# Means over the features in the head norms: one full fp32 matmul, or two one-pass matmuls of two exact parts

## The chip, the cores and the metric

The kernel runs on one core of one Trainium2 chip. The metric is the device time of one execution in microseconds (us). The engines are TensorE (PE in the profile; PEld is its weight load), VectorE (DVE), ScalarE (ACT), GpSimd (POOL) and SyncE (SP). Each engine works through its own instructions strictly in program order and waits on semaphores where an instruction needs another engine's result.

## The reference, cut to what matters

One inference step of a decoder layer with 512 prompt tokens and 8 decoding tokens, 2048 features, all in fp32. One projection gives the columns of three head groups: A, an HGRN2 recurrence (4 heads); B, sliding-window attention (8 heads); C, a retention (4 heads). Groups A and C end in a norm over the 128 features of a head, times a gate:

```python
def head_rms_norm(o, g):                       # group A
    y = o * lax.rsqrt(jnp.mean(o * o, axis=-1, keepdims=True) + NORM_EPS)
    return y * g

def head_group_norm(o, g):                     # group C
    c = o - jnp.mean(o, axis=-1, keepdims=True)
    y = c * lax.rsqrt(jnp.mean(c * c, axis=-1, keepdims=True) + NORM_EPS)
    return y * g

o_a = head_rms_norm(o_a, a_gain) * silu(ga)
o_c = head_group_norm(o_c, c_gain) * silu(gc)
mix = concatenate([o_a, o_b, o_c]); x = x + mix @ w_out
x = x + conv_ffn(rms_norm(x))                  # 2048 -> 2 x 5632 -> 2048
```

## The kernel before, in words

**Layout.** Features lie on the 128 partitions, tokens along the free dimension: 520 columns (512 prompt tokens and 8 decoding tokens), handled as two halves of 260. A mean over the features of a head is therefore a sum over partitions, done as a matmul with a 128x128 matrix of 1/128 (`onesV`).

**Projection gemms.** All large matmuls use three one-pass matmuls of operands that are split in a high part (`hi`, rounded to fp32r) and the exact rest (`lo`). A weight slab is 4 x 128 rows by 256 columns. `Slabs` loads it by DMA (SP queue), ScalarE makes `hi` (L157), VectorE makes `lo` (L159). `Slabs.next()` runs when a slab's matmuls are about to be issued, and splits two slabs ahead; there are three buffers for `hi` and three for `lo`. `zgemm` runs `gemm_pair` over four slabs; a slab is 2 x 24 matmuls of 260 columns, the first 24 for output block j = 0 and the others for j = 1 (L186, L188, L190). After the last slab's half j, `evac(j)` moves the PSUM accumulator to a tile `z` on VectorE (L324). There are two accumulators (`pg`), one for each j, so that the first matmul of the next gemm waits until `z` for j = 0 has been read out.

**Background work.** What is not a projection runs as Python generators in the list `bg`. `step()` advances each generator by one `yield`; `gemm_pair` calls it once after each slab and, for the slabs in `twice`, also between the halves (j = 0 done, j = 1 not). `drain()` runs all that is left. The order of the instructions on every engine is the order in which they are issued here; there is no other scheduler. So a step's instructions stand, on each engine, between the gemm's instructions of that place, and in front of the next slab's split.

**Pairs.** Groups A and C run as pairs of heads, `hgrn_pair(0)`, `hgrn_pair(2)`, `ret_pair(0)`, `ret_pair(2)`, below the first and second HGRN pair and the first and second retention pair. A pair is appended to `bg` when its four projections are done, gets one step at once, and then runs beside the four gemms of the next pair (4, 4, 4 and 6 steps, the fourth with `twice` = slabs 0 and 2); then comes `drain()`. The last pair runs beside the attention's projections KB (8 steps), VB (4) and QB (4), and after its `drain()` the pool `wk` of work tiles is closed (L643) and the attention's pool `wb` takes its place: the constants `c_bias` and others are loaded into it by GpSimd's DMA queue (L650 to L657), `kv_tokens` transposes (PSUM tiles `ptt`, `pl`, `pn`, copied to `vtb`, `plast`, `kvnew`), and `swa_pair` starts with the scores (`psc`, L703), the softmax (L706 to L721, with `c_bias`) and, one step later, the transposes of its result (`ppt`, L693).

**The head norm.** `head_norm` is the end of each pair: for group C first the mean of `o` and its subtraction (L453); then the square (L456, tile `x`), a `yield`, the mean of the square with the epsilon added (L460, tile `v`), Ln and Exp (L462, L463), a `yield`, a Newton step (L214 to L216) and the gains (L467), a `yield`, the gate product (L469) and its high part (L470), a `yield`, and the low part (L472; tiles `mla`, `mlc`). In an HGRN pair the mean of the square is issued in the middle of the third slab of the fourth gemm, Newton and the gains after that slab, the gate product and the high part after the fourth slab, the low part in `drain()`. In the first retention pair the mean of `o` comes after the third gemm and the mean of the square in the middle of the first slab of the fourth; in the second retention pair the mean of `o` comes after VB and the mean of the square after QB's first slab.

**Small PSUM tiles.** All other matmul results (`mn` of the means, the transposes `ptt`, the retention scores `pa` and so on) share four PSUM buffers (`pmt`). The work tiles with tags "k" and "c" have one buffer each; `k` and `c` of an HGRN pair and `v` of the head norm live there.

The first step of an HGRN pair transposes `zi` (`ptt`, copied to `vt`, L384) and starts the gate's logarithm (L501 to L506); its second and third step are L508 to L511 and L515 to L517; the fourth ends with L521 and L523. The first step of a retention pair has only transposes and copies (`vt` L384, `kdt` L386); its second starts with the scores `pa` (L605).

Of the kernel before, what the change touches and what calls it, by code (L numbers as in the profile page):

```python
# [9 lines left out]
F32 = mybir.dt.float32  # L10
F32R = mybir.dt.float32r
U8 = mybir.dt.uint8
AF = mybir.ActivationFunctionType
ALU = mybir.AluOpType
# [3 lines left out]
P = 128  # L18
D = 2048
T = 512  # L20
NB = 8
TT = T + NB
# [46 lines left out]
def hybrid_step(ctx: ExitStack, tc: tile.TileContext, I: dict, C: dict, O: dict):  # L69
    nc = tc.nc  # L70
    V, S, G, PE = nc.vector, nc.scalar, nc.gpsimd, nc.tensor
    ctx.enter_context(tc.manual_schedule())

    def pool(name, bufs=1, **kw):
        return ctx.enter_context(tc.tile_pool(name=name, bufs=bufs, **kw))

    const = pool("const")
# [6 lines left out]
    def pmt(name):  # L84
        return pm.tile([P, 512], F32, tag="pm", name=name)
# [29 lines left out]
    nc.sync.dma_start(ident, C["ident"])  # L115
    gv = const.tile([P, 60], F32, name="gv")
    onesD = const.tile([P, P], F32, name="onesD")
    onesV = const.tile([P, P], F32, name="onesV")
    epst = const.tile([P, 1], F32, name="epst")
    rbc1 = const.tile([P, TT], F32, name="rbc1")  # L120
    V.memset(onesD, 1.0 / D)
    V.memset(onesV, 1.0 / P)
    V.memset(epst, EPS)
    G1, G2, GF, HG, RG, LB = 0, 16, 32, 48, 52, 56

# [86 lines left out]
    def newton(r, v, t):  # L212

        V.tensor_tensor(t, r, r, op=ALU.mult)  # L214
        V.scalar_tensor_tensor(t, t, -0.5, v, op0=ALU.mult, op1=ALU.mult)
        V.scalar_tensor_tensor(r, t, 1.5, r, op0=ALU.add, op1=ALU.mult)  # L216
# [32 lines left out]
    for nm, r in (("norm2_g", 16), ("final_norm_g", 16), ("hgrn_norm_g", 4), ("ret_norm_g", 4), ("hgrn_lb_raw", 4)):  # L249
        src = I[nm] if nm == "final_norm_g" else I[nm][0]  # L250
# [15 lines left out]
    for q in range(4):  # L266
        hi, lo, src = x1h[q][:, :, T:TT], x1l[q][:, :, T:TT], xsg[:, 4 * q:4 * q + 4]
# [88 lines left out]
    def work(shape, tag, bufs=1, dt=F32):  # L356
        return wk.tile(shape, dt, tag=tag, name=tag, bufs=bufs)
# [83 lines left out]
    def head_norm(o, sg, gains, mh, ml, center):  # L441

        def mean(src):
            ps = [pmt("mn") for _ in range(3)]
            for j in range(2):
                PE.matmul(ps[j], onesV, src[:, j, 0:T], start=True, stop=True)
            PE.matmul(ps[2][:, 0:2 * NB], onesV, src[:, :, T:TT], start=True, stop=True)
            return [(ps[0], slice(0, 1), slice(0, T)), (ps[1], slice(1, 2), slice(0, T)),
                    (ps[2][:, 0:2 * NB].rearrange("p (j b) -> p j b", j=2), slice(0, 2), slice(T, TT))]

        if center:
            for ps, js, cs in mean(o):
                V.tensor_tensor(o[:, js, cs], o[:, js, cs], ps if js.stop - js.start == 2 else ps.unsqueeze(1),  # L453
                                op=ALU.subtract)
        sq = work([P, 2, TT], "x", 2)
        S.activation(sq, o, AF.Square)  # L456
        yield
        v = work([P, 2, TT], "c")
        for ps, js, cs in mean(sq):
            S.activation(v[:, js, cs], ps if js.stop - js.start == 2 else ps.unsqueeze(1), AF.Identity, bias=epst)  # L460
        r = work([P, 2, TT], "x", 2)
        S.activation(r, v, AF.Ln)  # L462
        S.activation(r, r, AF.Exp, scale=-0.5)  # L463
        yield
        newton(r, v, sq)
        for j in range(2):
            V.scalar_tensor_tensor(o[:, j], o[:, j], gains[j], r[:, j], op0=ALU.mult, op1=ALU.mult)  # L467
        yield
        V.tensor_tensor(o, o, sg, op=ALU.mult)  # L469
        S.activation(mh, o, AF.Copy)  # L470
        yield
        V.tensor_tensor(ml, o, mh.bitcast(F32), op=ALU.subtract)  # L472
# [23 lines left out]
    def hgrn_pair(hh, zf, zi, sg, zq, mh, ml):  # L496
# [91 lines left out]
        read_out(o, vt, att, kdt, q)  # L588
        yield
        yield from head_norm(o, sg, [gv[:, HG + hh + j:HG + hh + j + 1] for j in range(2)], mh, ml, False)  # L590

    def ret_pair(hh, zk, zv, sg, zq, mh, ml):
        vt = [work([P, 4, P], "vt", 2) for _ in range(2)]
        to_tokens(zv, vt)
        kdt = [work([P, 4, P], "kdt", 2) for _ in range(2)]
        to_tokens(zk, kdt, [tail[:, hh + j:hh + j + 1] for j in range(2)])
        o = work([P, 2, TT], "o")
        bg.insert(0, samples(hh, zq, zk, zv, GAMMA[hh:hh + 2], DK_SCALE, I["state_ret"], O["s_ret"], o))
        yield
        att = work([P, 2, 4, P], "att")  # L600
        for j in range(2):
            pa = pmt("pa")
            for ch in range(4):
                s = slice(ch * P, (ch + 1) * P)
                PE.matmul(pa[:, s], zk[:, j, s], zq[:, j, s], start=True, stop=True)  # L605
            V.tensor_tensor(att[:, j], chunks(pa),
                            dmat[:, hh + j, :].unsqueeze(1).to_broadcast([P, 4, P]), op=ALU.mult)
        for j in range(2):
            qv = chunks(zq[:, j, 0:T])
            V.tensor_tensor(qv, qv, inner[:, hh + j, :].unsqueeze(1).to_broadcast([P, 4, P]), op=ALU.mult)  # L610
        yield
        state_chain(kdt, vt, lambda j, ch: GAMMA[hh + j] ** P, [O["p_ret"][0, 0, hh + j] for j in range(2)])
        yield
        read_out(o, vt, att, kdt, zq)
        for _ in range(9):
            yield
        yield from head_norm(o, sg, [gv[:, RG + hh + j:RG + hh + j + 1] for j in range(2)], mh, ml, True)
# [1043 lines left out]
```

## Time and profile before

| what | value |
|---|---|
| median of 3 runs | 2287.44 us (2286.61 to 2291.74) |
| profiled execution, its own time | 2289.31 us |
| its span, first to last instruction | 2287.5 us |
| mean granted TensorE clock | 0.996 |
| matmul instructions | 18052 |

The profile is of one execution. A row of its timeline gives start, length, engine, line, operation, output and input tile, shapes, and in brackets the idle time of the engine before it and what ended it; several like instructions are merged into one row (x2). Matmuls are pipelined, so that the distance between starts, not the length, says what one costs. An fp32 matmul appears as two records, a one-pass matmul (fp32r operands) as one. The head norms lie between 219 and 555 us.

### The profile page before, as it was taken

What the parts mean: (1) busy time and instruction counts of PE and PEld (TensorE: products, weight loads), DVE (VectorE), ACT (ScalarE), POOL (GpSimd) and SP (SyncE); (2) the same over time, 40 slices, a digit from 0 to 9 for tenths busy, and PEclk for the clock granted to TensorE, in tenths of its full rate; (3) what the DMA queues carried; (4) which work ended last, traced back from release to release, by engine and by line L of the source; (5) the groups of instructions that cost most, each with busy time, mean ns of one, the idle gap of its engine ahead of it and who ended that gap; (6) DMA issues with size and microseconds to landing.
All of it is one profiled execution on the core that took longest, in us unless ns stands there. A gap on an engine that the chain in (4) does not pass through costs nothing.

```text
span 2287.5 us, 42302 instructions
## 1 busy us (share of the span) xinstructions
PE 2248.2 (98%) x18052; PEld 2213.2 (97%) x18052; DVE 1581.8 (69%) x2108; ACT 949.5 (42%) x1331; POOL 200.4 (9%) x424
## 2 busy tenths in 40 slices
PE   8999999999999999899999999999999999999996
PEld 8999999999999998899999999999999999999996
DVE  4265664444553448888888889888887887887446
ACT  6234332223352343544444454545444433434225
POOL 0001020111010110000000000000001000000002
PEclk9999999999999999999999999999999999999998
DMA  5323232234233443343433443433445446545523
GB/s 187 105 84 95 79 100 91 89 114 132 83 128 105 136 123 116 102 131 105 128 118 106 131 120 113 121 115 118 121 128 185 153 134 216 171 133 192 195 66 130
DMA packets 355019, 285.72 MB, mean 125 GB/s; under 512 B 9196, under 2 KB 336712, under 8 KB 353760
## 3 DMA queue, kind: packets, MB, share of 16 engines
q1 hardware_dynamic: 335728, 216.82, 31.5%
q0 software_dynamic: 19104, 66.21, 8.0%
q8 instruction: 142, 2.33, 0.4%
q14 instruction: 45, 0.37, 0.0%
HBM read 248.77 MB, written 36.64 MB: 125 GB/s over the span
## 4 chain that ended last, share of the span: by engine, by line
PE 70%; DVE 5%; ACT 1%; issue 1%; DMA 1%; ACTq 0%; DVEq 0%; POOLq 0%
PE pw L1227 15%; PE pw L1228 15%; PE pw L1229 15%; PE pw L972 9%; PE pg L186 3%; PE pg L190 3%; PE pg L188 3%; PE pw L1199 2%; DVE lo L936 1%; PE pw L1235 1%; ACT hi L934 1%; DMA r<-in_w_down 1%; PE psc L703 1%; PE pob L685 1%; DVE t L1325 0%
## 5 line engine op out<-in xcount | busy, mean ns | idle before, releaser
L934 ACT ACTIVATE hi<-r 128x1024 fp32r<-128x1024 f32 x208 | 220.4, 1060 | 282.8 <-PE pw L1228 186.9
L936 DVE TENSOR_TENSOR lo<-s,hi 128x1024 fp32r<-128x1024 f32 x224 | 273.7, 1222 | 87.0 <-ACT hi L934 85.2
L934 ACT ACTIVATE hi<-s 128x1024 fp32r<-128x1024 f32 x224 | 237.0, 1058 | 174.5 <-PE pw L1228 165.9
L186 PE MATMUL pg<-x1h,hi 128*128 128x260 f32 x1408 | 290.1, 287 | 3.0 <-ACT hi L157 1.7
L936 DVE TENSOR_TENSOR lo<-r,hi 128x1024 fp32r<-128x1024 f32 x208 | 260.5, 1253 | 44.7 <-ACT hi L934 44.7
L190 PE MATMUL pg<-x1h,lo 128*128 128x260 f32 x1408 | 284.2, 283 | 0.0
L188 PE MATMUL pg<-x1l,hi 128*128 128x260 f32 x1408 | 283.6, 283 | 0.0
L159 DVE TENSOR_TENSOR lo<-raw,hi 128x1024 fp32r<-128x1024 f32 x104 | 127.1, 1222 | 168.2 <-ACT hi L157 156.7
L186 PEld LDWEIGHTS pg<-x1h,hi 128*128 128x128 f32 x1408 | 217.7, 189 | 4.5 <-ACT hi L157 2.1
L190 PEld LDWEIGHTS pg<-x1h,lo 128*128 128x128 f32 x1408 | 217.3, 189 | 0.3 <-DVE lo L159 0.3
L188 PEld LDWEIGHTS pg<-x1l,hi 128*128 128x128 f32 x1408 | 217.4, 189 | 0.0
L1092 DVE SCALAR_TENSOR_TENSOR cv<-u,convc,cv 128x512 f32<-128x512 f32 (+1 forms) x176 | 132.0, 751 | 44.0 <-ACT cv L1087 43.9
L1227 PE MATMUL pw<-b22h,hi 128*128 128x260 f32 x448 | 126.8, 283 | 5.2 <-DVE u L1142 3.0
L1227 PE MATMUL pw<-b21h,hi 128*128 128x260 f32 x448 | 127.8, 285 | 0.0
L1227 PE MATMUL pw<-t4h,hi 128*128 128x260 f32 x448 | 127.6, 285 | 0.0
L157 ACT ACTIVATE hi<-raw 128x1024 fp32r<-128x1024 f32 x104 | 109.6, 1056 | 43.1 <-PE pg L188 36.6
L1227 PE MATMUL pw<-t1h,hi 128*128 128x260 f32 x448 | 127.1, 284 | 0.0
L1228 PE MATMUL pw<-t3l,hi 128*128 128x260 f32 x448 | 127.1, 284 | 0.0
L1228 PE MATMUL pw<-t1l,hi 128*128 128x260 f32 x448 | 127.0, 284 | 0.0
L1228 PE MATMUL pw<-t2l,hi 128*128 128x260 f32 x448 | 127.0, 283 | 0.0
L1227 PE MATMUL pw<-t3h,hi 128*128 128x260 f32 x448 | 127.0, 283 | 0.0
L1228 PE MATMUL pw<-t4l,hi 128*128 128x260 f32 x448 | 126.9, 283 | 0.0
(446 smaller groups left out, 6353.7 us busy)
## 6 DMA issues: line engine op xcount, KB each, us to landing
r<-in_w_up SPq DMA_DIRECT2D x88, 1024.0 KB, 5.3
raw<-in_w_in SPq DMA_DIRECT2D x88, 512.0 KB, 3.6
r<-in_w_down SPq DMA_DIRECT2D x40, 1024.0 KB, 5.7
agd<-cv POOLq DMA_DIRECT2D x16, 520.0 KB, 3.5
g<-agd POOLq DMA_DIRECT2D x8, 1040.0 KB, 10.7
cv<-x2d POOLq DMA_DIRECT2D x16, 520.0 KB, 6.9
x2d<-cv POOLq DMA_DIRECT2D x16, 520.0 KB, 6.2
raw<-in_w_out SPq DMA_DIRECT2D x16, 512.0 KB, 3.5
```

The source lines that it names most:

```text
L157: S.activation(hi, raw, AF.Copy)
L159: V.tensor_tensor(lo, raw, hi.bitcast(F32), op=ALU.subtract)
L186: PE.matmul(ps[:, i, 0:b - a], wh, xh[:, a:b], start=first, stop=False)
L188: PE.matmul(ps[:, i, 0:b - a], wh, xl[:, a:b], start=False, stop=False)
L190: PE.matmul(ps[:, i, 0:b - a], wl, xh[:, a:b], start=False, stop=last)
L934: S.activation(hi, view, AF.Copy)
L936: V.tensor_tensor(lo, view, hi.bitcast(F32), op=ALU.subtract)
L972: PE.matmul(ps[t][:, 0:b - a], wt[:, kk], x[:, a:b], start=kk == 0 and wt is hi and x is xh, stop=kk == nk - 1 and wt is lo)
L1092: V.scalar_tensor_tensor(cv[:, j, 0:w], u[:, j, i:i + w], convc[:, i, n], cv[:, j, 0:w], op0=ALU.mult, op1=ALU.add)
L1227: PE.matmul(ps(k), hi[:, m], xh[:, m], start=a, stop=False, skip_group_check=True)
L1228: PE.matmul(ps(k), hi[:, m], xl[:, m], start=False, stop=False, skip_group_check=True)
L1229: PE.matmul(ps(k), lo[:, m], xh[:, m], start=False, stop=z, skip_group_check=True)
```

## The change

The mean is now computed on two parts of its input: `hi`, rounded to fp32r by ScalarE, and `lo`, the exact rest from VectorE, each multiplied in one pass by an fp32r matrix of 1/128 and summed in the same PSUM accumulators. `mean` becomes a generator with a `yield` between the split and the matmuls. The parts use the work tiles' tags "k" and "c". The fp32r matrix is made by one ScalarE copy at the start.

```diff
-    onesV = const.tile([P, P], F32, name="onesV")
+    onesR = const.tile([P, P], F32R, name="onesR")
...
-    V.memset(onesV, 1.0 / P)
+    S.activation(onesR, onesD, AF.Copy, scale=float(D // P))
...
         def mean(src):
+
+            hi, lo = work([P, 2, TT], "k", dt=F32R), work([P, 2, TT], "c", dt=F32R)
+            S.activation(hi, src, AF.Copy)
+            V.tensor_tensor(lo, src, hi.bitcast(F32), op=ALU.subtract)
+            yield
             ps = [pmt("mn") for _ in range(3)]
-            for j in range(2):
-                PE.matmul(ps[j], onesV, src[:, j, 0:T], start=True, stop=True)
-            PE.matmul(ps[2][:, 0:2 * NB], onesV, src[:, :, T:TT], start=True, stop=True)
+            for x in (hi, lo):
+                for j in range(2):
+                    PE.matmul(ps[j], onesR, x[:, j, 0:T], start=x is hi, stop=x is lo)
+                PE.matmul(ps[2][:, 0:2 * NB], onesR, x[:, :, T:TT], start=x is hi, stop=x is lo)
...
-            for ps, js, cs in mean(o):
+            for ps, js, cs in (yield from mean(o)):
...
-        for ps, js, cs in mean(sq):
+        for ps, js, cs in (yield from mean(sq)):
```

## The prediction

> **What bounds the kernel now.** I read the page's head first, then the busy time by stage, then the waits of TensorE in the stage that holds the head norms, and last that stage's instructions in order of time.
>
> ```profile
> span 2287.5 us, 42302 instructions
> PE 2248.2 (98%) x18052; PEld 2213.2 (97%) x18052; DVE 1581.8 (69%) x2108; ACT 949.5 (42%) x1331; POOL 200.4 (9%) x424
> ```
>
> By stage (length; then busy time and instructions of TensorE, its weight loads, VectorE, ScalarE and GpSimd; then granted clock and DMA):
>
> ```profile
> 200.00:300.00 100.00, 98.95 (x824) 97.38 (x824) 59.42 (x90) 39.76 (x57) 11.71 (x19) 1.00 0.29 90
> 500.00:600.00 100.00, 99.75 (x789) 96.60 (x790) 46.57 (x91) 31.55 (x64) 13.90 (x23) 1.00 0.38 121
> ```
>
> All that TensorE waits for between 215 and 620 us (total, times, longest):
>
> ```profile
> PE pg L186 <- DVE z L324: 1.3, 3, 0.6
> PE pq L425 <- DVE si L437: 0.2, 1, 0.2
> ```
>
> TensorE issues without a pause here, so every microsecond of matmul removed shortens the span, and every new pause of TensorE lengthens it. VectorE and ScalarE are half idle on average, but each works strictly in program order; what counts is what stands in front of the next instruction that TensorE needs. The profiled execution took 2289.31 us around its 2287.5 us span; the median shown is 2287.44. All terms below are differences, which I add to the median.
>
> **The matmuls removed.** One mean now, in TensorE's order:
>
> ```profile
> 222.27 0.41 PE L190 MATMUL pg<-x1h,lo 128*128 128x260 f32 x2
> 222.51 1.88 PE L446 MATMUL mn<-x,onesV 128*128 128x512 f32 x4
> 224.23 0.29 PE L447 MATMUL mn<-x,onesV 128*128 128x16 f32 x2
> 224.37 0.49 PE L186 MATMUL pg<-x1h,hi 128*128 128x260 f32 x2
> 224.69 0.28 PE L188 MATMUL pg<-x1l,hi 128*128 128x260 f32 x1
> ```
>
> From start to start the three fp32 matmuls take 224.37 - 222.51 = 1.86 us, and the pair behind the short ones takes 0.32 instead of 0.24 us: 1.94 us in all. The four wide records take 0.43 us each. No one-pass matmul of 512 columns is in the trace. From below it is half a record, 0.215 us; from above it is scaled from the one-pass 260 columns (a pair in 0.24, so 0.12 each): 0.12 x 512/260 = 0.24 us. The short ones take 0.07 each, and each leaves 0.08 behind it. After: 4 x 0.215 + 2 x 0.07 + 2 x 0.08 = 1.16, at most 1.26 us. The saving is 0.68 to 0.78 us a mean, and there are six means (one in each HGRN pair, two in each retention pair): 4.1 to 4.7 us. I take 0.77, by the record nearest in width. [...]
>
> The constant costs one small ScalarE instruction in the start-up, where ScalarE idles for 5.19 us; that idle time hides it:
>
> ```profile
> 7.20 0.59 ACT L268 ACTIVATE x1h<-xsg 128x32 fp32r<-128x32 f32 x4 [5.19 <-DVE xsg L265]
> ```
>
> **What it adds.** Each mean gets a 128x1040 ScalarE copy, a 128x1040 VectorE subtract, and a yield, so everything behind it runs one background step later. The copy (1.07 us like L470 below) and the subtract (1.24, like L472) are themselves hidden: they stand a step, 2.9 to 5.8 us, ahead of the matmuls. The shift is the cost. The path from the first matmul of a variance to the end of Exp is 5.0 us now (222.51 above to 226.42 + 1.08 below), and I keep it: the matmuls are 0.8 us shorter, but v shares its one buffer with the low part and can start only behind the last matmul.
>
> *First HGRN pair.* Rows of VectorE, ScalarE and TensorE:
>
> ```profile
> 227.53 1.24 DVE L214 TENSOR_TENSOR x<-x 128x1040 f32<-128x1040 f32 x1 [4.30 <-PE pg L190]
> 233.84 1.30 DVE L324 TENSOR_TENSOR z<-pg,rbc 128x520 f32<-128x520 f32 x2
> 235.06 1.23 DVE L469 TENSOR_TENSOR o<-o,z 128x1040 f32<-128x1040 f32 x1
> 237.43 1.24 DVE L472 TENSOR_TENSOR mla<-o,mha 128x1040 fp32r<-128x1040 f32 x1 [1.14 <-ACT mha L470]
> 243.82 1.23 DVE L159 TENSOR_TENSOR lo<-raw,hi 128x1024 fp32r<-128x1024 f32 x1 [3.19 <-ACT hi L157]
> 256.46 1.23 DVE L159 TENSOR_TENSOR lo<-raw,hi 128x1024 fp32r<-128x1024 f32 x1 [1.23 <-ACT hi L157]
> 257.61 1.29 DVE L324 TENSOR_TENSOR z<-pg,rbc 128x520 f32<-128x520 f32 x2
> ```
> ```profile
> 226.42 1.08 ACT L463 ACTIVATE x<-x 128x1040 f32<-128x1040 f32 x1
> 236.32 1.07 ACT L470 ACTIVATE mha<-o 128x1040 fp32r<-128x1040 f32 x1 [7.88 <-DVE o L469]
> 242.75 1.99 ACT L157 ACTIVATE hi<-raw 128x1024 fp32r<-128x1024 f32 x2
> ```
> ```profile
> 233.10 1.03 PE L382 MATMUL ptt<-c_ident,z 128*128 128x128 f32 x8
> 234.59 0.50 PE L186 MATMUL pg<-x1h,hi 128*128 128x260 f32 x2 [0.46 <-DVE z L324]
> 258.45 0.47 PE L186 MATMUL pg<-x1h,hi 128*128 128x260 f32 x2 [0.57 <-DVE z L324]
> ```
>
> The mean moves from the middle of the gemm's last slab but one to its end: 222.51 + 24 x 0.12 = 225.4. Exp ends at 230.4; the next slab's copy (1.0) and lo (1.2) follow, and at 232.5 the pair of z evacuations, which takes 1.2. Only then, at 233.7, does Newton begin; it now stands ahead of that split and of the evacuations. Newton and the gains take 235.06 - 227.53 - 1.2 (evacuations) - 1.1 (split) = 5.2 us, so the gate product comes at 238.9 instead of 235.06: 3.8 us later. From there all hangs together without slack: high part, low part, the next pair's first Exp and Ln, the copy at 242.75, lo at 243.82, the six Exp and Ln of the next step, lo at 256.46, z at 257.61, TensorE at 258.45. TensorE first loses at the third slab of the next gemm: it now needs lo at 234.59 + 11.6 = 246.2 and has it at 245.05, a slack of 1.2 us against 3.8. At 258.45 it already waits for z. **Net +3.8 us**, matmul saving included.
>
> *Second HGRN pair.* The same times plus 121.8 us; the next pair is a retention pair, whose first step has no VectorE work:
>
> ```profile
> 356.82 1.23 DVE L469 TENSOR_TENSOR o<-o,z 128x1040 f32<-128x1040 f32 x1
> 359.06 1.05 ACT L384 COPY vt<-ptt 128x512 f32<-128x512 f32 x2
> 362.40 1.95 PE L605 MATMUL pa<-z 128*128 128x128 f32 x16
> ```
>
> The two vt copies move to 362.9; the first ends at 363.45. The retention scores (pa) take the PSUM buffer that it frees, the fourth of four in rotation. TensorE would stand there at 362.40 - 0.77 = 361.6, and goes on at 363.5. **Net +1.1**, or -0.8 if another buffer is free.
>
> *First retention pair.* Two yields; the tail moves into the last two slabs of its gemm:
>
> ```profile
> 442.32 1.88 PE L446 MATMUL mn<-x,onesV 128*128 128x512 f32 x4
> 464.39 1.91 PE L382 MATMUL ptt<-c_ident,z 128*128 128x128 f32 x16
> ```
>
> The first mean takes the place of the second less one mean of now (442.32 - 1.94 = 440.4); the second follows after 1.2 us of matmuls and a slab and a half (72 x 0.12), at 450.2. Exp ends at 455.2, the split of the next slab at 457.4; Newton and gains take 5.2, gate product and high part end at 464.9, the following copy and lo at 467.1, and z frees the accumulator at 467.9. The transposes now start at 464.39 and the next gemm some 1.8 us later, at 466.2. After, TensorE would be there at 450.2 + 1.2 + 96 x 0.12 + 1.8 = 464.7, so it waits 3.2 us. **Net +1.7** (0.5 to 2).
>
> *Second retention pair.* Behind its last instruction the work pool closes, and the attention's constants are loaded into its place:
>
> ```profile
> 553.04 1.23 DVE L472 TENSOR_TENSOR mlc<-o,mhc 128x1040 fp32r<-128x1040 f32 x1
> 560.94 0.42 DVE L706 SCALAR_TENSOR_TENSOR pe<-psc,c_bias 128x256 f32<-128x256 f32 x1 [2.43 <-DMA sinks<-in_swa_sinks]
> 563.73 0.42 DVE L721 TENSOR_TENSOR pe<-pe,st 128x256 f32<-128x256 f32 x1
> ```
> ```profile
> 555.04 0.57 POOL L650 DMA_DIRECT2D c_bias<-const_bias  x1 [37.88 <-DVE mlc L472]
> ```
> ```profile
> 552.22 1.04 PE L382 MATMUL ptt<-c_ident,z 128*128 128x128 f32 x8
> 565.70 0.38 PE L693 MATMUL ppt<-c_ident,pe 128*128 128x128 f32 x2
> ```
>
> The last slab starts at 552.22 - 48 x 0.12 = 546.4 now. In front of it two means go (3.9) and one comes back (1.2), so the second mean starts there at 543.8. Exp ends at 548.8, split and evacuations at 552.2, Newton and gains at 557.4, low part at 559.7 instead of 553.04: 6.7 later. The bias load, queued on GpSimd behind it with ten small loads, moves by as much, and with it L706 and L721, to 570.9. TensorE's transposes of the softmax wait for that: 565.70 becomes 570.9. Part of it may be lost a slab earlier, where the scores need a PSUM buffer that the vtb copies, also held by mlc, give free. **Net +5.2** (6.5 if the load lands later; -1.5 if it does not wait for mlc).
>
> Sum: 3.8 + 1.1 + 1.7 + 5.2 = 11.8; 2287.4 + 11.8 = 2299 us. Behind 600 us nothing starts by the clock, so nothing gives it back.
>
> **The rivals.**
> *Cover holds (faster).* The weight splits lead by two slabs, 11.6 us; if the tail's delay stays below the slack of 1.2 us at 246.2, and the bias load is not held, only the matmuls count: -6 x 0.77 and -1.0 for the z waits of 0.46 and 0.57: 2282 us. The 50% idle VectorE speaks for it, the in-order rows above against it. Chance 0.07.
> *The bias load is not held.* Its row blames mlc, but a 0.77 us gap lies between mlc's end and its issue. Then the last pair gives -1.5: 3.8 + 1.1 + 1.7 - 1.5 = +5.1, 2292.5 us. Chance 0.13.
> *Half cover.* The second HGRN pair keeps -0.8 and the first loses only 2.5, the retention pairs 0.5 and 1: about +3, 2290.5 us. Chance 0.12.
> *The clock drops behind the new pauses.* In the start-up, matmuls run slow:
>
> ```profile
> 11.84 0.80 PE L186 MATMUL pg<-x1h,hi 128*128 128x260 f32 x2 [1.72 <-ACT hi L157]
> 15.85 0.40 PE L190 MATMUL pg<-x1h,lo 128*128 128x260 f32 x2
> 930.00:934.00 4.00, 2.33 (x20) 2.13 (x18) 4.00 (x4) 0.85 (x2) 0.72 (x2) 1.00 1.09 350
> ```
>
> 18 matmuls in 4.0 us there, where 18 x 0.12 = 2.2 would do: 1.8 us a drop. Two pauses of about 3 us would make it 11.8 + 3.6: 2303 us. Against it, TensorE idled 1.7 of 4 us from 930 at a clock of 1.00. Chance 0.08. [...]
>
> **How the numbers follow.** The forecast has the remaining 0.60: 2295 to 2303 us. A range of 2289 to 2303 leaves out the cover rival, part of half cover and the upper tail. 0.2% is 4.6 us, about what a measurement can tell: the bounds are 2282.9 and 2292.0. Slower: 0.60 + 0.08 + half of 0.13 = 0.75. Same: 0.12 and the other half, 0.18. Faster: 0.07.
>
> **What would show it.** Mean: six matmul records in about 1.2 us. First HGRN pair: the third slab behind it waits 3 us for hi and lo, Newton starts behind z. First retention pair: L186 waits some 3 us for z near 465. Last: c_bias issued some 6 us later against the gemm's end, transposes ppt waiting for L721. If TensorE is as busy as now from 200 to 600 us, the forecast is wrong.

## The result, and the profile after

The changed kernel takes 2301.88 us (median of 6, 2301.04 to 2304.10) against 2288.45 us before (median of 6): the ratio is 1.0059, with a 95% interval of 1.0048 to 1.0070. It is 13.4 us slower. The span of its profiled execution is 2299.2 us against 2287.5; single executions of one kernel differ by some 5 us.

The head of the page, and the same stages as before (length; busy time of TensorE, its weight loads, VectorE, ScalarE, GpSimd; granted clock, DMA):

```profile
span 2299.2 us, 42316 instructions
PE 2251.9 (98%) x18052; PEld 2220.4 (97%) x18052; DVE 1588.5 (69%) x2113; ACT 956.7 (42%) x1339; POOL 200.9 (9%) x424
```
```profile
200.00:300.00 100.00, 96.02 (x790) 94.91 (x790) 59.00 (x87) 39.82 (x56) 10.35 (x17) 0.98 0.27 84
500.00:600.00 100.00, 95.88 (x752) 94.14 (x752) 46.19 (x84) 30.86 (x58) 16.85 (x27) 0.97 0.37 118
```

The page's head shows almost nothing: TensorE is busy 98% as before. The loss is in the stages: TensorE falls from 98.95 to 96.02 us of the hundred from 200, and from 99.75 to 95.88 from 500, and the clock, which was 1.00, is 0.98 and 0.97. What TensorE waits for from 215 to 620 us (total, times, longest) was 1.5 us in two rows before. Now:

```profile
PE pg L186 <- DVE z L324: 4.3, 3, 3.1
PE psc L709 <- ACT vtb L384: 3.6, 1, 3.6
PE pg L186 <- ACT hi L157: 2.8, 1, 2.8
PE pa L611 <- ACT vt L384: 1.8, 1, 1.8
PE pq L425 <- DVE si L437: 0.2, 1, 0.2
PE pg L190 <- DVE lo L159: 0.2, 1, 0.2
```

Each of the four pairs has left its own wait: hi for the first HGRN pair, pa for the second, z (the 3.1) for the first retention pair, psc for the second. To size them I compared when TensorE starts the same instruction in both traces:

| TensorE starts | before | after | difference | lost by the pair |
|---|---|---|---|---|
| ptt, ahead of all head norms | 200.52 | 200.25 | -0.27 | |
| pa behind the first HGRN pair | 266.06 | 269.62 | 3.56 | 3.83 |
| pk behind the second HGRN pair | 369.94 | 374.76 | 4.82 | 1.26 |
| pst behind the first retention pair | 474.14 | 482.15 | 8.01 | 3.19 |
| ppt behind the second retention pair | 565.70 | 578.54 | 12.84 | 4.83 |

The four add up to 13.1 us. TensorE stays 12.8 us late up to 935 us on the scale of before; behind that the order of waits and clock changes differs between the two profiled executions (mean clock 0.96 before and 0.97 after from 2100 us) and gives some 1 us back, so that the spans differ by 11.7.

TensorE's rows of one mean and of the waits:

```profile
225.12 0.62 PE L452 MATMUL mn<-k,onesR 128*128 128x512 f32 x2
225.58 0.17 PE L453 MATMUL mn<-k,onesR 128*128 128x16 f32 x1
225.60 0.71 PE L452 MATMUL mn<-c,onesR 128*128 128x512 f32 x2
226.15 0.17 PE L453 MATMUL mn<-c,onesR 128*128 128x16 f32 x1
226.18 0.49 PE L186 MATMUL pg<-x1h,hi 128*128 128x260 f32 x2
...
247.41 0.60 PE L186 MATMUL pg<-x1h,hi 128*128 128x260 f32 x2 [2.78 <-ACT hi L157]
261.97 0.47 PE L186 MATMUL pg<-x1h,hi 128*128 128x260 f32 x2 [0.95 <-DVE z L324]
...
367.12 2.05 PE L611 MATMUL pa<-z 128*128 128x128 f32 x16 [1.80 <-ACT vt L384]
...
472.57 0.48 PE L186 MATMUL pg<-x1h,hi 128*128 128x260 f32 x2 [3.08 <-DVE z L324]
...
569.67 1.23 PE L709 MATMUL psc<-z 128*128 128x128 f32 x4 [3.62 <-ACT vtb L384]
578.54 0.39 PE L699 MATMUL ppt<-c_ident,pe 128*128 128x128 f32 x2
```

(`...` marks rows left out.) The mean does become cheaper: 226.18 - 225.12 = 1.06 us, and 0.08 behind it, against 1.94. VectorE's rows show what that costs around the first HGRN pair:

```profile
232.13 1.30 DVE L324 TENSOR_TENSOR z<-pg,rbc 128x520 f32<-128x520 f32 x2
233.34 1.23 DVE L214 TENSOR_TENSOR x<-x 128x1040 f32<-128x1040 f32 x1
238.62 1.24 DVE L475 TENSOR_TENSOR o<-o,z 128x1040 f32<-128x1040 f32 x1
247.39 1.23 DVE L159 TENSOR_TENSOR lo<-raw,hi 128x1024 fp32r<-128x1024 f32 x1 [3.18 <-ACT hi L157]
261.13 1.30 DVE L324 TENSOR_TENSOR z<-pg,rbc 128x520 f32<-128x520 f32 x2
```

Newton (L214) stands behind z, at 233.34 where it was at 227.53. The gate product comes at 238.62 instead of 235.06, lo at 247.39 instead of 243.82, z at 261.13 instead of 257.61: the same 3.5 to 3.6 us through the whole chain.

Behind the second retention pair, GpSimd and VectorE:

```profile
569.55 0.57 POOL L656 DMA_DIRECT2D c_bias<-const_bias  x1 [45.15 <-issue]
```
```profile
567.63 1.24 DVE L478 TENSOR_TENSOR mlc<-o,mhc 128x1040 fp32r<-128x1040 f32 x1 [1.14 <-ACT mhc L476]
575.07 0.42 DVE L712 SCALAR_TENSOR_TENSOR pe<-psc,c_bias 128x256 f32<-128x256 f32 x1 [2.03 <-DMA c_bias<-const_bias]
577.86 0.43 DVE L727 TENSOR_TENSOR pe<-pe,st 128x256 f32<-128x256 f32 x1
```

The bias load is issued 0.7 us behind the end of mlc, VectorE waits for it, and the softmax (L727) ends at 578.29, a quarter of a microsecond before TensorE transposes it. TensorE itself does not wait there: it has spent the time one slab earlier, in the wait of the scores for vtb and in the slow matmuls behind that wait (granted clock 0.57 from 568 to 572 us).

### The profile page after: what moved, and what is told of

Same layout as the page of the kernel before. It is cut to its first block, busy times and chain, and to the rows that moved or that the text cites. A ratio compares the mean times of both kernels' runs of the same rounds, so it can differ in the third digit from the quotient of the medians.

```text
span 2299.2 us, 42316 instructions
## 1 busy us (share of the span) xinstructions
PE 2251.9 (98%) x18052; PEld 2220.4 (97%) x18052; DVE 1588.5 (69%) x2113; ACT 956.7 (42%) x1339; POOL 200.9 (9%) x424
## 4 chain that ended last, share of the span: by engine, by line
PE 69%; DVE 5%; ACT 2%; issue 1%; DMA 1%; ACTq 0%; POOL 0%; DVEq 0%; SPq 0%; POOLq 0%
PE pw L1233 15%; PE pw L1234 15%; PE pw L1235 15%; PE pw L978 9%; PE pg L186 3%; PE pg L188 3%; PE pg L190 3%; PE pw L1205 3%; PE pw L1241 1%; DVE lo L942 1%; ACT hi L940 1%; PE psc L709 1%; PE pob L691 1%; DVE n L1317 0%; DMA x<-x2d 0%
## 5 line engine op out<-in xcount | busy, mean ns | idle before, releaser
L186 PEld LDWEIGHTS pg<-x1h,hi 128*128 128x128 f32 x1408 | 219.8, 191 | 10.8 <-ACT hi L157 5.1
L1235 PE MATMUL pw<-b22h,lo 128*128 128x260 f32 x448 | 128.0, 286 | 0.0
L1234 PE MATMUL pw<-b22l,hi 128*128 128x260 f32 x448 | 126.9, 283 | 0.0
```

The source lines that it names most:

```text
L186: PE.matmul(ps[:, i, 0:b - a], wh, xh[:, a:b], start=first, stop=False)
L1234: PE.matmul(ps(k), hi[:, m], xl[:, m], start=False, stop=False, skip_group_check=True)
L1235: PE.matmul(ps(k), lo[:, m], xh[:, m], start=False, stop=z, skip_group_check=True)
```

## The experiments

The theory: what costs is the place of the norm's tail, which each new yield moves by a step. Rivals: the added work on ScalarE and VectorE; and, for part of it, TensorE's clock behind the new waits. "Lost by the pair" below is read as in the table above. Each kernel ran on the same chip as runs of the kernel before; those had medians of 2289.2 to 2289.5 us.

**A bare yield, nothing else (e1_yield_only).**

```diff
 (before)  def mean(src):
+            yield
             ps = [pmt("mn") for _ in range(3)]
```

> The kernel before with its fp32 matmuls and no split; only a bare yield stands in front of the matmuls of each mean. Theory (the shift of the tail by one step per mean is the cost): the first HGRN pair loses the same 3.8 us, the second 1.1 to 1.9, the first retention pair 3.2 and the second 4.8, the last two plus 0.8 each since the fp32 mean in front is longer: 13 to 16 us slower than before, 2302 to 2304. Rival (the added ScalarE copy and VectorE subtract are the cost): no more than 2 us slower than before.

Measured: 2305.99 us against 2289.45, ratio 1.0074 (1.0061 to 1.0088), 16.5 us slower. The pairs lose 4.2, 1.5, 4.0 and 5.7 us. TensorE's waits are those of the changed kernel:

```profile
PE pg L186 <- DVE z L324: 3.2, 3, 2.3
PE psc L704 <- ACT vtb L384: 3.1, 1, 3.1
PE pg L186 <- ACT hi L157: 2.4, 1, 2.4
PE pa L606 <- ACT vt L384: 1.3, 1, 1.3
```

The yield alone, without any split work, makes all of the loss and more. The 4.8 us that the one-pass matmuls save (6 x 0.80) are seen only as 16.5 - 13.4 = 3.1 us, or 15.4 - 13.1 = 2.3 us by the pairs. My reading, which no run isolates: in the shifted tail, chains of VectorE set the end in part.

**The split without the yield (e2_no_yield).**

```diff
 (after)     V.tensor_tensor(lo, src, hi.bitcast(F32), op=ALU.subtract)
-            yield
             ps = [pmt("mn") for _ in range(3)]
```

> The changed kernel without the yield between the split and the matmuls. Theory: the tail is back at its old steps, but TensorE now stands at each mean until copy and subtract are done; worked out from the rows of before: first HGRN pair +1.1, second +0.4, first retention pair +5.4 (the copy stands behind the gate's two table loads), second +0.6: 7.5 us slower than before, up to 9.5 if the clock drops behind the wait of over 4 us, and so faster than the changed kernel by 4 to 6 us. Rival (only the yield costs): 4.6 us faster than before. Rival (the split work costs wherever it stands): as slow as the changed kernel.

Measured: 2302.13 us against 2289.45, ratio 1.0056 (1.0041 to 1.0072), 12.7 us slower: as slow as the changed kernel, by other waits. The pairs lose 1.3, 1.2, 8.2 and 0.0 us, 10.6 in sum. TensorE and ScalarE at the first retention pair:

```profile
450.72 1.22 PE L451 MATMUL mn<-k,onesR 128*128 128x512 f32 x2 [5.07 <-ACT k L446]
```
```profile
444.98 1.28 ACT L626 ACT_TABLE_LOAD   x1
446.27 1.07 ACT L626 ACTIVATE z<-z 128x1040 f32<-128x1040 f32 x1
447.36 1.28 ACT L97 ACT_TABLE_LOAD   x1
448.65 1.06 ACT L157 ACTIVATE hi<-raw 128x1024 fp32r<-128x1024 f32 x1
449.62 1.05 ACT L446 ACTIVATE k<-x 128x1040 fp32r<-128x1040 f32 x1
```

The place was foreseen, the size not: the copy stands behind the gate's two table loads and a weight split, TensorE waits 5.07 us, and behind it runs at a clock of 0.50 from 452 to 456 us. Without a yield the split has no cover. In the profiled execution another 2.5 us are lost far behind the norms, between 2128 and 2249 us: TensorE waits 1.86 us for VectorE at 2142.14, and the clock is at 0.57 from 2142 to 2146 us. Whether that belongs to the change is not shown.

**The split work alone, its result unused (e3_split_unused).**

```diff
 (before)  def mean(src):
+            hi, lo = work([P, 2, TT], "k", dt=F32R), work([P, 2, TT], "c", dt=F32R)
+            S.activation(hi, src, AF.Copy)
+            V.tensor_tensor(lo, src, hi.bitcast(F32), op=ALU.subtract)
```

> The kernel before with its fp32 matmuls, and the copy and the subtract of the split issued in front of them without a yield; their results are not used. Theory (only the order matters): VectorE and ScalarE have room at these places, within 1 us of before. Rival (the added ScalarE and VectorE work costs): six times 2.3 us or a good part of it, 5 to 14 us slower.

Measured: 2291.72 us, ratio 1.0012 (1.0003 to 1.0021), 2.3 us slower (0.7 to 4.8 by the interval); more than the 1 us expected, and far from 13. The pairs lose 0.55, 0.4, 0.9 and 0.0. VectorE and ScalarE at the first HGRN pair:

```profile
223.21 1.23 DVE L446 TENSOR_TENSOR c<-x,k 128x1040 fp32r<-128x1040 f32 x1
228.21 1.24 DVE L214 TENSOR_TENSOR x<-x 128x1040 f32<-128x1040 f32 x1 [3.77 <-ACT x L466]
```
```profile
224.53 1.43 ACT L463 ACTIVATE c<-mn,epst 128x512 f32<-128x512 f32 x3 [1.54 <-PE mn L449]
```

The variance (c, 224.53) starts when the low part is written (223.21 + 1.23 = 224.44), not at 223.57 as before, when the first mean was ready: both live in the one buffer "c". So Newton comes at 228.21 instead of 227.53. Work that an idle engine does for nothing is not free when its tile shares a buffer.

**As many more steps as yields (e4_more_steps).**

```diff
 (after)
-            sg = gate(zgemm(cols[2] + hh))
+            sg = gate(zgemm(cols[2] + hh, twice=(0,)))
-        for _ in range(9):
+        for _ in range(8):
-    zk, zv = zgemm(KB, twice=(0, 1, 2, 3)), zgemm(VB)
+    zk, zv = zgemm(KB, twice=(0, 1, 2, 3)), zgemm(VB, twice=(0,))
```

> The changed kernel, with as many more background steps as it has more yields: one step more between the halves of the first slab of the third gemm of each pair (and of VB for the last pair), and 8 waiting yields instead of 9 in the retention pairs. All of the tail behind the matmuls stands where it stood before. Theory: the loss is gone and the matmuls' saving shows where no chain of VectorE sets the end: first HGRN pair 0 (z still late), second -0.8, retention pairs -1.6 each: 4 us faster than before, 2284.5. Rival (the two-part mean costs more than it saves, wherever it stands): slower than before by 5 us or more.

Measured: 2287.53 us, ratio 0.9994 (0.9985 to 1.0003). The 13 us are gone: with the same split work, the same matmuls and the tail at its old steps the kernel is as fast as before. Of the expected gain of 4 us some 2 are missing: TensorE waits 1.6 us for the samples' state (pq for si) where the additional step leaves VectorE only half a slab, and 1.2 us for z behind the first HGRN pair.

**The additional step elsewhere (e8_late_steps):** `twice=(3,)` in both gemms in place of `twice=(0,)`.

> As e4_more_steps, with the additional step put between the halves of the fourth slab of the third gemm (and of VB) instead of the first, where the samples' matmuls no longer stand too close behind VectorE (their 1.6 us of waits in e4). Theory: first HGRN pair 0, second -0.6, retention pairs -1.6 each: 3.5 to 4 us faster than before. Rival: as e4, 1 to 2 us faster, if the waits come from somewhere else.

Measured: 2288.74 us, ratio 0.9994 (0.9985 to 1.0003). The rival: pq's wait falls to 0.3 us, but the transposes of kd now come half a slab behind VectorE's product and wait 0.9 us in each HGRN pair. At both places half a slab between a producer and its consumer was too little.

**The last pair alone (e7_last_pair):** the changed kernel with `zgemm(VB, twice=(2, 3))`.

> The changed kernel with two more background steps for the last pair alone (between the halves of VB's third and fourth slab), so that the second retention pair's tail stands where it stood before, and the other three pairs stay shifted. Theory: the 4.8 us at the transposes of the softmax go, and the pair gains the 1.6 us of its two means: 6.4 us faster than the changed kernel, about 7 us slower than before; the wait of the scores for vtb is gone and the clock stays at 1.00 around 570 us. Rival (the pair's loss comes from the split work): as slow as the changed kernel.

Measured: 2296.66 us against 2289.22, ratio 1.0034 (1.0022 to 1.0045), 7.4 us slower. TensorE reaches the softmax's transposes at 572.28 instead of 578.54; the wait for vtb is gone; the clock is 1.00 from 552 to 576 us. The last pair gains 1.4 us instead of losing 4.8. GpSimd's row names what holds the load:

```profile
561.63 0.57 POOL L656 DMA_DIRECT2D c_bias<-const_bias  x1 [36.89 <-DVE mlc L478]
```

In the changed kernel it was issued at 569.55, 8 us later. This run frees vtb and the load together; no run frees one alone.

**Keeping TensorE busy in one wait (e5_warm).**

```diff
 (after)  def ret_pair(hh, zk, zv, sg, zq, mh, ml):
+        if hh:
+            warm = pmt("warm")
+            for _ in range(24):
+                PE.matmul(warm[:, 0:HALF], onesR, x1h[0][:, 0, 0:HALF], start=True, stop=True)
```

> The changed kernel with 24 one-pass matmuls of 260 columns, their result unused, in front of the transposes of the second retention pair: 2.9 us of work in the 3.1 us in which TensorE otherwise waits for z behind the first retention pair. Theory (part of that pair's 3.2 us is the clock, which the profile of the changed kernel shows at 0.62 in the 4 us behind this wait): the granted clock stays at 1.00 there and the pair loses 1.7 us instead of 3.2, so 1.5 us faster than the changed kernel, 12 us slower than before. Rival (the clock falls for another reason, or the wait alone is the loss): as slow as the changed kernel, or slower by the later transposes.

Measured: 2300.06 us against 2289.22, ratio 1.0048 (1.0033 to 1.0064); 10.8 us slower, where the changed kernel was 13.4 slower against its own runs of before. The first retention pair loses 1.6 us instead of 3.2. First the changed kernel from 472 us, then this one:

```profile
472.00:476.00 4.00, 3.43 (x17) 3.46 (x18) 3.31 (x4) 1.63 (x3) 0.00 (x0) 0.62 0.40 131
```
```profile
472.00:476.00 4.00, 3.80 (x33) 3.59 (x32) 3.67 (x5) 2.56 (x4) 0.00 (x0) 1.00 0.45 131
```

17 matmuls in the 4 us behind the wait against 33: with useless matmuls in the wait the clock stays at 1.00, and TensorE starts the next gemm at about the same time (472.84; 472.57 in the changed kernel) but runs it at full speed. In e7_last_pair, where the wait is still there (3.07 us), the clock falls again, to 0.62 from 473 to 477 us. Half of this pair's loss is the clock.

The last pair is worth a look here too:

```profile
577.60 0.41 PE L703 MATMUL ppt<-c_ident,pe 128*128 128x128 f32 x2 [0.83 <-ACT hi L157]
```

TensorE comes to the transposes earlier, in front of the end of the softmax (L731, 577.39), and now waits 0.8 us. The profile names the weight split hi, which ScalarE runs behind its own part of that softmax. In e1_yield_only it is the same, with 0.6 us.

**Shortening the chain that sets the first HGRN pair.** Two moves of VectorE work in the HGRN pairs: the gains behind the z evacuations, and the low part of the output (L472) away from the front of the next pair's first step. First with the low part on GpSimd (e9_gains_pool):

```diff
 (e8_late_steps)  newton(r, v, sq)
+        if not center: yield
         ...gains...
+        if center: yield
-        V.tensor_tensor(ml, o, ...)
+        (V if center else G).tensor_tensor(ml, o, ...)
```

> As e8_late_steps, and in the HGRN pairs the gains move behind the z evacuations (into the step of the gate product) and the low part goes from VectorE to GpSimd, which stands idle there. Theory: the chain from the first HGRN pair's Newton step to z at 258 us loses 2.3 us of VectorE, both z waits (1.2 at 234.5, 0.5 at 258) go and the pair gains its 0.8 and these: 1.3 to 1.8 us faster than e8, 5 to 6 us faster than before. Rival (GpSimd slows VectorE where both work, or the chain is bound by ScalarE): no faster than e8.

Measured: 2287.27 us, ratio 0.9992 (0.9983 to 1.0000). No more than e4 and e8 gave; the rival. GpSimd's and VectorE's rows:

```profile
237.94 2.45 POOL L481 TENSOR_TENSOR mla<-o,mha 128x1040 fp32r<-128x1040 f32 x1 [27.50 <-ACT mha L479]
```
```profile
237.39 3.55 DVE L513 SCALAR_TENSOR_TENSOR x<-x,z 128x520 f32<-128x520 f32 x2
```

While GpSimd subtracts, VectorE's two instructions take 3.55 us; they took 1.31 before. The 2.3 us saved are lost again at once, and TensorE still waits 1.78 us for z, at 258.70. So the low part stays on VectorE but is issued later, in the next pair's second or third step, where VectorE idles; first on the kernel before, with its fp32 means (e11_before_moved):

```diff
 (before)  head_norm, HGRN pairs
-        V.tensor_tensor(ml, o, mh.bitcast(F32), op=ALU.subtract)
+        late.append(low)              # low() is this subtract
 (hgrn_pair, end of its third step; ret_pair, end of its second)
+        while late:
+            late.pop()()
```

> The kernel before, with its fp32 means, and two moves of VectorE work in the HGRN pairs: the gains go behind the z evacuations, and the low part of the norm's output is issued two to three background steps later, where VectorE idles. Theory (the first HGRN pair is set by a chain of VectorE work from the Newton step to z at 258 us): the chain loses 2.3 us, and the two z waits of 0.5 and 0.6 us go: 1 us faster than before. Rival (the waits come from ScalarE's part): no change.

Measured: 2287.24 us, ratio 0.9989 (0.9980 to 0.9998), 2 us faster than before (1 was expected); the first HGRN pair gains 1.5 us by the trace. With the two-part mean, the additional steps (`twice=(0,)` in the third gemms, `twice=(3,)` in VB, 8 waiting yields) and the two moves (e12_late_low):

> The changed kernel with the additional background steps (first slab of the third gemm as in e4_more_steps, fourth slab of VB as in e8_late_steps, 8 waiting yields), and the two moves of e11_before_moved. Theory: nothing of a tail stands late, so that the matmuls' saving is seen in all four pairs: -1.8, -0.6, -1.6, -1.6 and 0.6 of waits at the additional steps: 4.5 to 5.5 us faster than before, and 3.5 to 4.5 faster than e11_before_moved. Rival (the split work on ScalarE and VectorE, 2.3 us in e3_split_unused, stays in the path): 2 to 3 us faster than before.

Measured: 2284.26 us (median of 11) against 2289.30, ratio 0.9976 (0.9968 to 0.9985): 5.0 us faster than before, as the theory said, and 3.0 faster than e11_before_moved on the same chip, a little less than the 3.5 to 4.5 expected. VectorE around the first HGRN pair:

```profile
233.11 1.30 DVE L324 TENSOR_TENSOR z<-pg,rbc 128x520 f32<-128x520 f32 x2
234.33 1.42 DVE L477 SCALAR_TENSOR_TENSOR o<-o,gv,x 128x520 f32<-128x520 f32 x2
247.49 1.24 DVE L484 TENSOR_TENSOR mla<-o,mha 128x1040 fp32r<-128x1040 f32 x1
255.90 0.69 DVE L324 TENSOR_TENSOR z<-pg,rbc 128x520 f32<-128x520 f32 x1
```

Gains behind z, the low part at 247.49 in a gap, and z at 255.90 ahead of TensorE, which has no wait for z here any more. This version beats both the kernel before and the changed one.

**The split behind the square, without a step of its own (e13_split_early).**

```diff
 (after)   S.activation(sq, o, AF.Square)
+        hl = split2(sq)                     # copy and subtract, without a yield
         yield
-        for ps, js, cs in (yield from mean(sq)):
+        for ps, js, cs in mean(*hl):
```

and the same for `o`, in place of one of the nine waiting yields.

> The changed kernel without a yield of its own: the split of the square is issued right behind the square, in front of the yield that is there anyway, and the split of o takes the place of one of the nine waiting yields. The tail stays at its old steps. Theory: TensorE waits 0.4 us for the low part in each HGRN pair and 1.5 in the first retention pair; 0, -0.4, -0.1, -1.6: 2 us faster than before. Rival (the split must stand a step ahead): slower than before by 3 us or more.

Measured: 2288.58 us, ratio 0.9998 (0.9989 to 1.0006). As fast as before; TensorE waits 1.9 us for the two parts, in the two HGRN means and the second mean of the first retention pair, which takes most of the rest of the gain.

## Why the prediction was right, point by point

The forecast was 2299 us, in a range of 2289 to 2303; 2301.88 were measured. The bare yield shows that the mechanism is the one forecast: the shift of the tail makes the loss without any split work. e4 shows that nothing of the loss is left once the shift is undone.

- **Matmuls.** A saving of 0.77 us a mean was forecast (0.68 to 0.78) and 0.80 measured (1.94 - 1.14). A wide one-pass matmul takes 0.23 us, between the two bounds (0.215 and 0.24); the short ones take 0.02 to 0.03 instead of 0.07. The lower bound was half a record by assumption, which no run shows; the measured pass lies 0.015 us above it.
- **First HGRN pair.** 3.8 forecast, 3.83 measured, with the same row late at each point: gate product 238.62 (238.9 forecast), z 261.13. The path of 5.0 us from matmul to Exp, kept because v shares a buffer, was right: the matmuls start at 225.12, Exp ends at 228.93 + 1.07 = 230.0, 4.9 us later, and e3 shows that shared buffer holding v.
- **Second HGRN pair.** 1.1 forecast, 1.26 measured, and at the forecast place: pa waits 1.80 us for the vt copies. That the scores need the buffer which the copy frees was inferred from four buffers in rotation; the wait bears it out.
- **First retention pair.** 1.7 forecast, 3.2 measured: the term that was mis-sized. Its wait is 3.08 us (3.2 forecast), but the clock behind it was left out; e5 gives 1.6 us back by filling the wait. The prediction had the clock as a rival, with 1.8 us a drop from slow matmuls in the start-up, where the profile of before shows a granted clock of 1.00 (12 to 16 us); no run shows 1.8 us for a drop of the clock, and filling this wait in e5 gave back 1.6. It gave the rival 0.08, because TensorE idled 1.7 of the 4 us from 930 at a clock of 1.00. That window holds only the first part of one unbroken wait of 2.99 us, and 8 us later comes another of 3.12 us (rows below). The clock stayed at 1.00 behind the first and fell to 0.57 behind the second, so the trace of before spoke for both outcomes and gave no ground for a chance as low as 0.08.
- **Second retention pair.** 5.2 forecast, 4.8 measured. The late low part, the late load and the late softmax are as forecast, and in e1 and e5 TensorE waits at the transposes, as the prediction said it would. In the changed kernel it does not: it loses 3.62 us at the scores, which the prediction named as possible, and 2.7 us more between the scores and the transposes (8.87 us instead of 6.18), where the clock is low (0.50 from 570 to 574 us). It then arrives just as the softmax ends. That the softmax's chain would have cost about as much without the low clock is inferred from e1 and e5, not tested by itself.
- **Sum.** 11.8 forecast, 13.1 by the trace; the clock's 1.5 us in the first retention pair are most of the difference. The measured 2301.88 lies nearer to the rival with the clock (2303) than to the forecast (2299). That rival adds to the shift and does not replace it; the clock fell behind three of the new waits (to 0.61, 0.62 and 0.57 over 4 us), but by the trace only the one in the first retention pair adds its full price.
- **The split as such** was called hidden. Without a step of its own it costs 2.3 us (e3); in the changed kernel, where it has one, no wait of TensorE for the two parts is in the list above.

TensorE in the kernel before, at the place from which the prediction argued about the clock:

```profile
935.32 0.36 PE L1227 MATMUL pw<-b22h,hi 128*128 128x260 f32 x1 [2.99 <-DVE u L1142]
943.10 0.39 PE L1228 MATMUL pw<-b11l,hi 128*128 128x260 f32 x1 [3.12 <-ACT b11l L1374]
936.00:940.00 4.00, 3.98 (x34) 3.77 (x32) 4.00 (x5) 2.02 (x2) 0.00 (x0) 1.00 0.00 0
944.00:948.00 4.00, 4.00 (x23) 4.00 (x22) 3.54 (x4) 1.33 (x2) 0.00 (x0) 0.57 0.20 60
```

## What to carry to other kernels

In a hand-ordered interleave a yield is not free: it moves everything behind it past other work, on every engine's queue at once, and the price is set by what then stands in front of the next instruction that the bound engine needs. Count steps as a resource: a change that needs one more must be given one more, at a place where producer and consumer keep their distance (half a slab was too little at two places here). The matmuls' gain of 4.8 us was real, but it took an additional step and two moves off the chain to see 3.0 us of it (e12 against e11).

## What the runs showed of the hardware

The granted clock fell behind these waits of TensorE: 2.78 us (0.61 from 248 to 252 us), 3.08 (0.62 from 472 to 476) and 3.62 (0.57 from 568 to 572) in the changed kernel, and 5.07 (0.50 from 452 to 456) in e2. Behind the wait of 1.80 us for vt in the changed kernel it stayed at 1.00 (366 to 370 us). The length of the wait alone does not decide it. The wait for u near 935 us is 2.99 us in the kernel before, with a clock of 1.00 behind it (936 to 940 us), and 3.01 us in the changed kernel, with a clock of 0.50 behind it (948 to 952 us). In the 13 profiled executions this wait of 2.96 to 3.01 us is followed by a drop in seven and by none in six. The shortest wait that I found with a drop is 1.86 us (e2, 0.57 from 2142 to 2146 us). The clock also fell without a wait, in the kernel before, to 0.71 from 748 to 752 us, around and behind 32 matmuls of only 4 columns each:

```profile
746.29 3.74 PE L828 MATMUL pos<-sT,kv 128*128 128x4 f32 x32
```

While it was low, pairs of 260 columns started 0.43 us apart (249.27 and 249.70 in the changed kernel) instead of 0.24 (252.24 and 252.48). In slices of 2 us the clock was 0.92, 0.50 and 0.73 from 246 us, 0.74, 0.50 and 0.91 from 472 us, and 0.63, 0.50, 0.50 and 0.66 from 568 us. What is missing to 1.00, times 2 us, comes to 1.7 us in the first HGRN pair, 1.7 us in the first retention pair and 3.4 us in the last: an estimate from these slices. In the first retention pair, where TensorE is the bound, filling the wait gave 1.6 us back (e5). In the first HGRN pair the missing 1.7 us lie within VectorE's delay, 3.5 to 3.6 us at each of its rows, and by the trace add nothing to it.

In e9 a GpSimd subtract of 128x1040 (2.45 us) ran beside two VectorE instructions that took 3.55 us (at 237.39) instead of 1.31 (at 239.32 in the kernel before). It is one place in one run; in e12 the same two, without GpSimd beside them, took 1.31 us.
